# Mixture-of-experts stage: a new order of the expert units, gate-up weights stored in 4 KB runs, the next large unit's first two weight tiles split ahead of the down products, and the casts of y queued behind them

## The chip, the cores and the metric

The kernel runs on one core of a Trainium2 chip, in one launch. The metric is the device time of that launch in microseconds, the median over several runs. One further run was taken by the hardware profiler, and its trace is what all durations below come from. The engines are named as in the profile: PE is the matrix engine and PEld its weight load, DVE the vector engine, ACT the scalar engine, POOL and SP the other two; SPq is SP's queue of transfers.

## The reference

A block of transformer layers runs on 256 tokens of width 1024 in float32 (two feed-forward layers, a hybrid mixer, memory attention, convolution and differential attention). It ends with a mixture of experts, which the change is about:

```python
def moe_ffn(h, w_router, router_bias, w_gu, w_down, w_sh_gu, w_sh_down):
    ...
    _, eidx = lax.top_k(jnp.where(emask, choice, -jnp.inf), TOP_K)
    ...
    def chunk(args):
        tc, gc = args
        g, u = jnp.split(jnp.einsum('td,edf->tef', tc, w_gu), 2, axis=-1)
        return jnp.einsum('tef,efd->td', jax.nn.silu(g) * u * gc[..., None], w_down)
    ...
    sg, su = jnp.split(t @ w_sh_gu, 2, axis=-1)
    shared = (jax.nn.silu(sg) * su) @ w_sh_down
    return (routed + shared).reshape(B, S, D)
```

There are 64 experts of inner width 256, each token goes to 8 of them, and one shared expert takes all tokens. One expert has 2 MB of gate-up weights (1024 x 512) and 1 MB of down weights (256 x 1024).

## The kernel before, in words

The expert stage (`experts`) works through 27 units. A unit of kind L is one expert with up to 128 tokens; S is two experts with up to 64 tokens each; Q is four experts with up to 32 each (unit Q6 has two); the first, X, is three experts whose weights are known before the routing is done. Behind X come 14 L, 5 S and 7 Q units, 50 experts in all.

A unit multiplies its tokens `xe` by the gate-up weights into `eg` (eight slices of 128 rows, two to a tile), applies the gated activation (`glu`: `es` on ACT, then on DVE, and a transpose to `ehT` on PE), multiplies by the down weights into `y` (two halves `b` of 512 columns), and adds `y` to the four accumulators `acc`. That adding is a scatter by a 0/1 matrix `GT`: `y` is split into a high part `yh` (ACT) and a low part `yl` (DVE), and PE multiplies both, eight matmuls for a unit. They are kept in `self.left` and issued inside the next unit's `glu`, ahead of its transpose.

S and Q units use the float32 weights as they are. An L unit runs with split weights: ACT casts each tile of 1024 columns into `whi`, DVE subtracts it into `wlo` (`split`, by `wsplit`; four buffers of each), and PE does three matmuls for each slice (hi by hi, hi by lo, lo by hi: lines 2111 to 2113 for `eg`, 2124 to 2126 for `y`). For every second unit of a kind the tokens are gathered once for two units (`slots`, 32 matmuls `gx`, and `gg`, `GT`); the gather for unit q+1 is issued in unit q, between its transpose and its down products (`ahead`).

Weights arrive in tiles of 512 KB, six for an expert: four of gate-up and two of down (`expert_weights`, line 2054). A down tile is 128 rows of 4 KB; a gate-up tile has two runs of 2 KB for each partition, because its two slices lie 256 KB apart in memory. SP issues all of them in the order of the units, for the experts of a unit in turn, and waits where the buffer is not free. `raw` hands out the buffers in a fixed cycle of 20 (`RAW_N`), which is less than the 24 tiles of a Q unit. A tile of an S or Q unit is free when PE has read it, one of an L unit when both halves of its split are done.

The order of the units is computed from `SEQL`; it is X Q S Q L L S L Q L L Q L S L L Q L L S L Q L L L S Q. Behind the last unit the accumulators are scaled by `gB` and added to the residual, and the result is stored.

In program order a unit's weights are asked for and split at its own beginning, which is behind the casts of the unit before. The scheduler may move instructions of one engine against each other within the limits that `issue_after` sets.

Of the kernel before, what the change touches and what calls it, by code (L numbers as in the profile page):

```python
# [8 lines left out]
F32, F32R, I32 = dt.float32, dt.float32r, dt.int32  # L9
# [5 lines left out]
P = 128  # L15
# [6 lines left out]
NL, NS, NQ, NX = 14, 10, 26, 3  # L22
# [3 lines left out]
NRAW, WX, LB, LAST = 4, 6, 1, 4  # L26
CNORM = 1
ADA, ADA_BUFS, ADA_AHEAD = (10, 2), 3, 2
SEQL = (0.16, 0.7, 0.2, 0.0)

RAW_X = ["wx"] * WX + ["gB"] * 3 + ["xn"] * 3 + ["xel"] * 2 + ["xeh"] * 2 + ["xT"] * 2
RAW_1 = ["wraw"] * 2 + ["xT"] * 2 + ["wraw"] * 2
# [76 lines left out]
    return w.reshape(8, P, 1024)  # L109


def _freqs():
    import numpy as np

    return np.power(500000.0, -np.arange(0, 16, 2) / 16.0).astype(np.float32)[None]


class Net:
# [47 lines left out]
        return t  # L166

    def split(self, hi, lo, src, eng=None):
        self.nc.scalar.copy(hi, src)  # L169
        (eng or self.nc.vector).tensor_sub(lo, src, hi.bitcast(F32))  # L170

    def transpose_split(self, src, hi, lo, t, full=None):

# [134 lines left out]
    def wsplit(self, raw, eng=None, more=None):  # L308

        kc, n = raw.shape[1:]  # L310
        out = []
        st = min(kc, max(1, 1024 // n))
        for c in range(0, kc, st):
            if more is None:
                hi = self.whi.tile([P, st, n], F32R, name="whi", tag="whi")
                lo = self.wlo.tile([P, st, n], F32R, name="wlo", tag="wlo")
            else:
                hi, lo = [more[0].tile([P, st, n], F32R, name="wmore", tag=more[1], bufs=more[2]) for _ in range(2)]
            self.split(hi, lo, raw[:, c : c + st], eng)
            out += [(hi[:, i], lo[:, i]) for i in range(st)]  # L320
        return out

# [1722 lines left out]
    def expert_weights(self, es):  # L2045

        nc, A = self.nc, self.A
        out = [[] for _ in es]
        for i in range(6):
            for j, e in enumerate(es):  # L2050
                w = self.raw([P, 2, 512] if i < 4 else [P, 1, D])
                W, o = (A["w_exp_gu_2"], 2 * i) if i < 4 else (A["w_exp_down_2"], i - 4)
                src = W[0][bass.ds(e, 1)].rearrange("o (c p) n -> p (o c) n", p=P)
                dma = nc.sync.dma_start(w, src[:, o : o + w.shape[1]])
# [22 lines left out]
    def add_left(self):  # L2077
        left, self.left = self.left, []
        with self.tc.issue_after(self.last.ins):
            for f in left:  # L2080
                self.last = f()
# [7 lines left out]
    def scatter(self, y, b, GT, acc, last, r=P, first=False):  # L2089

        nc = self.nc
        yh, yl = self.ysplit(y, r)

        def add():
            for t in range(2):
                g = GT[:r, t * P : (t + 1) * P]
                nc.tensor.matmul(acc[t][b], g, yh, start=first, stop=False)  # L2097
                mm = nc.tensor.matmul(acc[t][b], g, yl, start=False, stop=last)  # L2098
            return mm

        self.left.append(add)

    def unit_L(self, w, xe, gate, put, ahead):
# [15 lines left out]
        with self.tc.issue_after(self.last.ins):  # L2119
            for b in range(2):  # L2120
                y = self.psum("y")
                o = slice(b * 512, b * 512 + 512)
                for c, (hi, lo) in enumerate(wd):
                    nc.tensor.matmul(y, hh[:, c], hi[:, o], start=c == 0, stop=False)
                    nc.tensor.matmul(y, hh[:, c], lo[:, o], start=False, stop=False)
                    nc.tensor.matmul(y, hl[:, c], hi[:, o], start=False, stop=c == 1)
                put(b, y)

    def unit_cols(self, pmT, gT, Sel, Off, tag):

# [16 lines left out]
        self.split(gU[:, :, :, 0], gU[:, :, :, 1], pv)  # L2147
        return Pu, gU

    def unit_multi(self, ws, n, xe, gate, put, ahead):  # L2150
# [11 lines left out]
        with self.tc.issue_after(self.last.ins):  # L2162
            for b in range(2):
                y = self.psum("y")
                for c in range(2):
                    for i, w in enumerate(ws):
                        o = slice(n * i, n * i + n)
                        nc.tensor.matmul(y[o], hT[:, c, o], w[4 + c][:, 0, b * 512 : b * 512 + 512],  # L2168
                                         start=c == 0, stop=c == 1)
                put(b, y)  # L2170

    def experts(self, h2t, U, fixed, shared):
        ids, Pu, gU = U["ids"], U["Pu"], U["gU"]
        nS, nQ = (NS + 1) // 2, (NQ + 3) // 4

        seq = [(SEQL[0] + (i + 0.5) / NL * SEQL[1], "L", i) for i in range(NL)]
        seq += [((i + SEQL[2]) / nS, "S", i) for i in range(nS)]

        seq += [((i + 1.0) / nQ if i < nQ - 1 else SEQL[3], "Q", i) for i in range(nQ)]
        seq = [("X", 0)] + [q[1:] for q in sorted(seq)]  # L2180
        first = dict(L=0, S=4 * NL, Q=Q0)
        cnt = dict(L=NL, S=nS, Q=nQ)
        ready = {("X", 0): U["X"]}

        def slots(q):

            if q == len(seq):
                return
            kind, i = seq[q]
            if i % 2 == 0:  # L2190
# [3 lines left out]
        self.left = []  # L2194

        def ahead(q):
            if q == 1:
                shared(acc)
            slots(q + 1)

        for q, (kind, i) in enumerate(seq):
            last = q == len(seq) - 1
            u0 = first.get(kind, 0) + 4 * i
# [3 lines left out]
            GTj, gate = GT[:, j], gs[:, j : j + 1]  # L2207
            if kind == "L":
                w = self.expert_weights(self.expert_ids(ids, [u0]))[0]
                self.unit_L(w, xj, gate, lambda b, y: self.scatter(y, b, GTj, acc, last), lambda: ahead(q))  # L2210
            else:
                n, k = dict(S=(64, min(NS - 2 * i, 2)), Q=(32, min(NQ - 4 * i, 4)), X=(32, NX))[kind]
                ws = fixed if kind == "X" else self.expert_weights(
                    self.expert_ids(ids, [u0 + n // 32 * v for v in range(k)]))
                self.unit_multi(ws, n, xj[0], gate,
                                lambda b, y: self.scatter(y, b, GTj, acc, last, n * k, q == 0), lambda: ahead(q))
        for f in self.left:
            f()
        self.left = []
# [2 lines left out]
    def overflow(self, h2t, U, gB):  # L2222
# [21 lines left out]
        with tc.For_i(0, total):  # L2244
# [33 lines left out]
            self.unit_L(w, [x[:, :, :P] for x in xe], gs[:, 0:1], put, lambda: None)  # L2278
            self.store()
            nc.vector.tensor_scalar(cnt, cnt, 1.0, None, ALU.add)  # L2280

# [43 lines left out]
norm2_g_2 w_router_2 router_bias_2 w_exp_gu_2 w_exp_down_2 w_sh_gu_2 w_sh_down_2""".split()  # L2325
_STAGES = ("ffn1", "mix", "mem", "ffn2", "blk", "moe")


# [21 lines left out]
```

## Time and profile before

| | |
|---|---|
| three runs | 1457.02, 1455.15, 1456.77 us; median 1456.77 us |
| the profiled execution | 1449.17 us |
| its span, first to last instruction | 1447.4 us |
| X unit's first matmul to the last scatter matmul's end | 1018.2 to about 1437.4 us |
| busy in the span: PE, DVE, ACT | 95%, 62%, 46% |
| SP queue's packets, as a share of 16 transfer engines' time | 70.8% |

The table is read from the profile's first page. Between the 1447.4 us of the span and the 1449.17 us of the execution lie 1.8 us outside the first and last instruction. The expert stage takes 419 us of the span, so its average is not that of the page: in that stretch the transfer engines are busy nearly all the time, and DVE less than half.

### The profile page before, as it was taken

How to read it: one execution, taken by the hardware profiler on the slowest of the kernel's cores; microseconds unless marked ns; L12 is line 12 of the kernel's file. 1: busy time of each engine (PE TensorE's matmuls, PEld its weight loads, DVE VectorE, ACT ScalarE, POOL GpSimd, SP SyncE). 2: the span in 40 equal slices, each digit the busy share in tenths (PEclk: the TensorE clock that was granted, in tenths of full speed). 3: DMA queues.
4: the chain of work that ended last, by engine and by line, in shares of the span. 5: the costliest groups of instructions: out<-in, count | busy, mean ns of one | idle time of the engine just before them, and what ended most of it. 6: DMA issues, size and time to landing. Idle time of an engine off the chain costs nothing.

```text
span 1447.4 us, 23621 instructions
## 1 busy us (share of the span) xinstructions
PE 1372.0 (95%) x8921; PEld 1078.0 (74%) x8921; DVE 899.2 (62%) x1420; ACT 666.2 (46%) x1051; POOL 128.1 (9%) x111
## 2 busy tenths in 40 slices
PE   6999999999999899999999989999999999989997
PEld 4999877898777679998798768776456575656572
DVE  4878465774457388664669987768226464645462
ACT  5445455545345354444453455843125353544351
POOL 1000012110101020000200314113000000000000
PEclk9999999999999999999999999999999999999999
DMA  7888566343245269875677543467989999999997
GB/s 263 293 301 288 191 205 206 98 138 103 74 161 185 78 229 309 271 245 184 201 238 219 153 130 89 159 211 270 372 299 395 394 390 396 391 392 385 340 383 266
DMA packets 175924, 358.00 MB, mean 247 GB/s; under 512 B 16099, under 2 KB 53931, under 8 KB 175807
## 3 DMA queue, kind: packets, MB, share of 16 engines
q1 hardware_dynamic: 175807, 356.46, 70.8%
q8 instruction: 71, 1.16, 0.3%
q14 instruction: 46, 0.38, 0.1%
HBM read 354.81 MB, written 1.60 MB: 246 GB/s over the span
## 4 chain that ended last, share of the span: by engine, by line
PE 55%; DVE 4%; ACT 3%; issue 1%; POOL 0%; DVEq 0%; POOLq 0%; ACTq 0%
PE eg L2158 6%; PE gx L2009 4%; PE y L2168 4%; PE lw L377 2%; PE eg L2112 2%; PE acc L2097 2%; PE lw L375 2%; PE lw L376 2%; PE eg L2113 2%; PE eg L2111 2%; PE acc L2098 2%; DVE wlo L170 2%; PE u L564 1%; PE g L565 1%; PE u L565 1%; PE g L564 1%
## 5 line engine op out<-in xcount | busy, mean ns | idle before, releaser
L170 DVE TENSOR_TENSOR wlo<-wraw,whi 128x1024 fp32r<-128x1024 f32 x262 | 323.3, 1244 | 120.7 <-ACT whi L169 119.5
L169 ACT CAST whi<-wraw 128x1024 fp32r<-128x1024 f32 x264 | 275.3, 1049 | 245.6 <-PE lw L377 54.8
L170 DVE TENSOR_TENSOR yl<-y,yh 128x512 fp32r<-128x512 f32 (+2 forms) x54 | 37.0, 689 | 74.9 <-ACT yh L169 74.9
L564 PE MATMUL u<-xTh,whi 128*128 128x256 f32 x288 | 82.1, 285 | 0.0
L2158 PE MATMUL eg<-wx,xe 128*32 128x512 f32 (+1 forms) x520 | 81.9, 594 | 0.0
L564 PE MATMUL g<-xTh,whi 128*128 128x256 f32 x288 | 81.6, 283 | 0.0
L565 PE MATMUL g<-xTl,whi 128*128 128x256 f32 x288 | 81.5, 283 | 0.0
L566 PE MATMUL g<-xTh,wlo 128*128 128x256 f32 x288 | 81.5, 283 | 0.0
L566 PE MATMUL u<-xTh,wlo 128*128 128x256 f32 x288 | 81.5, 283 | 0.0
L565 PE MATMUL u<-xTl,whi 128*128 128x256 f32 x288 | 81.5, 283 | 0.0
L170 DVE TENSOR_TENSOR wlo<-wx,whi 128x1024 fp32r<-128x1024 f32 x62 | 73.4, 1220 | 8.8 <-ACT whi L169 8.1
L1298 DVE SCALAR_TENSOR_TENSOR aacc<-wada,cc,aacc 128x1024 f32<-128x1024 f32 x48 | 61.5, 1281 | 18.2 <-DMA wada<-in_w_ada 17.5
L2066 DVE SCALAR_TENSOR_TENSOR es<-es,gsl,eg 128x256 f32<-128x256 f32 (+2 forms) x27 | 12.9, 479 | 85.5 <-ACT es L2065 85.5
L169 ACT CAST whi<-wx 128x1024 fp32r<-128x1024 f32 x62 | 63.1, 1051 | 5.2 <-PE eg L2113 3.2
L2158 PEld LDWEIGHTS eg<-wx,xe 128*32 128x32 f32 (+1 forms) x520 | 23.6, 117 | 50.7 <-issue 46.0
L169 ACT CAST yh<-y 128x512 fp32r<-128x512 f32 (+2 forms) x54 | 31.5, 586 | 62.6 <-PE y L2168 35.8
L2065 ACT ACTIVATE es<-eg 128x256 f32<-128x256 f32 (+2 forms) x27 | 10.4, 385 | 105.2 <-PE eg L2158 85.8
L2009 PE MATMUL gx<-G,h2h 128*128 128x256 f32 (+1 forms) x240 | 57.8, 284 | 0.0
L564 PEld LDWEIGHTS u<-xTh,whi 128*128 128x128 f32 x288 | 55.2, 192 | 3.4 <-ACT sf L537 1.7
L377 PE MATMUL lw<-whi,hl 128*128 128x512 f32 x144 | 56.7, 394 | 0.0
L2009 PE MATMUL gx<-G,h2l 128*128 128x256 f32 (+1 forms) x240 | 56.5, 278 | 0.0
L376 PE MATMUL lw<-wlo,hh 128*128 128x512 f32 x144 | 56.4, 392 | 0.0
(699 smaller groups left out, 3703.8 us busy)
## 6 DMA issues: line engine op xcount, KB each, us to landing
wx<-in_w_exp_gu SPq DMA_DIRECT2D x170, 512.0 KB
wx<-in_w_exp_down SPq DMA_DIRECT2D x86, 512.0 KB
wraw<-in_w_in SPq DMA_DIRECT2D x84, 512.0 KB
wada<-in_w_ada SPq DMA_DIRECT2D x48, 512.0 KB
wraw<-in_ffn_w_gate SPq DMA_DIRECT2D x44, 512.0 KB
wraw<-in_ffn_w_up SPq DMA_DIRECT2D x44, 512.0 KB
wraw<-in_ffn_w_down SPq DMA_DIRECT2D x44, 512.0 KB
wraw<-in_w_exp_gu SPq DMA_DIRECT2D x42, 512.0 KB
```

The costliest lines, as they stand in the source:

```text
L169: self.nc.scalar.copy(hi, src)
L170: (eng or self.nc.vector).tensor_sub(lo, src, hi.bitcast(F32))
L375: nc.tensor.matmul(o, x[0], w[0], start=start, stop=False)
L376: nc.tensor.matmul(o, x[0], w[1], start=False, stop=False)
L377: return nc.tensor.matmul(o, x[1], w[0], start=False, stop=stop)
L564: nc.tensor.matmul(p, hi, xh[:, k], start=k == 0, stop=False)
L565: nc.tensor.matmul(p, hi, xl[:, k], start=False, stop=False)
L566: mm = nc.tensor.matmul(p, lo, xh[:, k], start=False, stop=k == K - 1)
L1298: nc.vector.scalar_tensor_tensor(acc, w, self.cc[:, k : k + 1], acc, ALU.mult, ALU.add)
L2009: nc.tensor.matmul(ps[:, i * n : (i + 1) * n], h[:, t, f], G[:, t], start=j == 0, stop=j == 3)
L2158: mm = nc.tensor.matmul(ps[o], xe[:, k, o], w[k // 2][:, k % 2], start=k == 0, stop=k == 7)
L2168: nc.tensor.matmul(y[o], hT[:, c, o], w[4 + c][:, 0, b * 512 : b * 512 + 512], start=c == 0, stop=c == 1)
```

## The change

Four things change, all in the expert stage.

The **order** of the units is now written out as a string: X Q Q S L L Q L L S L L Q L S L Q L L L S L Q L S L Q. The numbers of units are the same.

**Gate-up weights** are passed to the kernel in another layout (`_pairs`): the two slices of a tile lie side by side, so that a tile is 128 rows of 4 KB, as a down tile is. The bytes are the same.

**A unit's weights are asked for in the unit before** (`then`, called ahead of the down products). If the next unit is an L, its first two gate-up tiles are split there as well, and the casts of this unit's `y` are issued behind those two splits (`split_first`).

**One of the four scatter pieces** (two matmuls) is held back until the transpose has been issued, in units behind which no gather follows (`behind`).

```diff
+SEQ = "QQSLLQLLSLLQLSLQLLLSLQLSLQ"
...
+def _pairs(w):
+    e, k, n = w.shape
+    return np.ascontiguousarray(w.reshape(e, k // 256, 2, P, n).transpose(0, 1, 3, 2, 4).reshape(e, k // 256, P, 2 * n))
...
     def expert_weights(self, es):
...
+                if i < 4:
+                    src = A["exp_gu"][bass.ds(e, 1), i].rearrange("o p (c n) -> p (o c) n", c=2)
...
     def glu(self, ps, mm, gate, r, ahead):
...
-        self.add_left()
+        self.add_left(len(self.left) - self.behind)
         pt = self.psum("ehT")
         with self.tc.issue_after(self.last.ins):
             for c in range(2):
                 self.last = nc.tensor.transpose(...)
+        self.add_left(len(self.left))
...
     def scatter(self, y, b, GT, acc, last, r=P, first=False):
-        yh, yl = self.ysplit(y, r)
+        with ExitStack() as es:
+            for i in self.split_first:
+                es.enter_context(self.tc.issue_after(i.ins))
+            yh, yl = self.ysplit(y, r)
...
+        self.left += [lambda t=t: add(t) for t in range(2)]
...
     def unit_L(self, w, ws, xe, gate, put, ahead, then):
         for k in range(0, 8, 2):
-            for i, (hi, lo) in enumerate(self.wsplit(w[k // 2])):
+            for i, (hi, lo) in enumerate(ws[k // 2] if k // 2 < len(ws) else self.wsplit(w[k // 2])):
...
         wd = self.wsplit(w[4]) + self.wsplit(w[5])
+        then()
+        for b in range(2):
+            with self.tc.issue_after(self.last.ins):
...
+            self.last = mm
+            put(b, y)
...
     def experts(self, h2t, U, fixed, shared):
...
+        def then(q):
+            self.split_first = ()
+            if q < len(seq):
+                kind, i = seq[q]
+                n, k = size(kind, i)
+                ws = self.expert_weights(self.expert_ids(ids, [...]))
+                weights[q] = ws, [self.wsplit(ws[0][v]) for v in range(2)] if kind == "L" else []
+                self.split_first = self.halved if kind == "L" else ()
         for q, (kind, i) in enumerate(seq):
+            self.behind = 0 if q < 2 or gathers(q + 1) else 1
+            ws, split = weights.pop(q)
...
```

How the change moves instructions is shown at three places. The first is ACT at the fourth full Q unit and the L unit behind it (Q3 and L8 in both orders). Before, from the Q unit's gather on:

```order
L2161 COPY ehT<-ehT 128x256
L169 CAST xeh<-gx 128x512 x4
L2035 CAST GT<-GT 128x512
L169 CAST yh<-y 128x512 x2
L169 CAST whi<-wx 128x1024 x6
L2065 ACTIVATE es<-eg 128x256
```

and now:

```order
L2177 COPY ehT<-ehT 128x256
L178 CAST xeh<-gx 128x512 x4
L2043 CAST GT<-GT 128x512
L178 CAST whi<-wx 128x1024 x2
L178 CAST yh<-y 128x512 x2
L178 CAST whi<-wx 128x1024 x4
L2075 ACTIVATE es<-eg 128x256
```

Two of the L unit's six casts stand ahead of the two casts of the Q unit's `y`, which PE has to finish first; DVE's subtractions stand in the same order.

The second is PE at the same L8 and the L9 behind it, where no gather stands between. Before, from the last scatter pieces to the first gate-up matmuls of L9:

```order
L2097 MATMUL acc<-yh,GT 128x512
L2098 MATMUL acc<-yl,GT 128x512
L2072 MATMUL ehT<-ident,es 128x128 x2
L2124 MATMUL y<-whi,ehh 128x512
L2125 MATMUL y<-wlo,ehh 128x512
L2124 MATMUL y<-whi,ehh 128x512
L2125 MATMUL y<-wlo,ehh 128x512
L2111 MATMUL eg<-whi,xeh 128x512
L2112 MATMUL eg<-wlo,xeh 128x512
L2126 MATMUL y<-whi,ehl 128x512
```

and now:

```order
L2082 MATMUL ehT<-ident,es 128x128 x2
L2111 MATMUL acc<-yh,GT 128x512
L2112 MATMUL acc<-yl,GT 128x512
L2139 MATMUL y<-whi,ehh 128x512
L2140 MATMUL y<-wlo,ehh 128x512
L2141 MATMUL y<-whi,ehl 128x512
L2139 MATMUL y<-whi,ehh 128x512
L2140 MATMUL y<-wlo,ehh 128x512
```

Two scatter matmuls stand between the transpose and the first product now, and the third product, which needs the low part `ehl`, stands third instead of fifth; L9's `eg` no longer stands among them.

The third is SP, at the weights of the X unit, up to the first load of an expert's number behind them. Before and now:

```order
L2054 DMA wx<-in_w_exp_gu 128x2x512 x2
L2054 DMA wx<-in_w_exp_down 128x1024 x2
L2054 DMA wx<-in_w_exp_gu 128x2x512 x6
L2054 DMA wx<-in_w_exp_down 128x1024 x4
L442 DMA wraw<-in_w_sh_down 128x1024 x2
L2039 TENSOR_LOAD ids
```

```order
L2064 DMA wx<-in_exp_gu 128x1024 x2
L2064 DMA wx<-in_w_exp_down 128x1024 x2
L2064 DMA wx<-in_exp_gu 128x1024 x6
L2064 DMA wx<-in_w_exp_down 128x1024 x4
L450 DMA wraw<-in_w_sh_down 128x1024 x2
L2047 TENSOR_LOAD ids
```

A gate-up tile is read as rows of 1024 words where it was two rows of 512; the order of the transfers changes only with that of the units.

## Rows read from the trace of the kernel before

**Rows 1.** Expert stage by --windows: length, busy of PE, PEld, DVE, ACT, POOL, PEclk, DMA, GB/s

```profile
1018.20:1437.40 419.20, 399.53 (x2285) 251.31 (x2285) 191.10 (x265) 164.39 (x249) 0.00 (x0) 0.99 1.00 375
```

**Rows 2.** PE's waits in the expert stage: us in total, times, longest

```profile
PE eg L2111 <- ACT whi L169: 7.6, 4, 2.2
PE eg L2112 <- DVE wlo L170: 3.8, 5, 0.8
PE y L2124 <- ACT ehh L169: 3.7, 8, 0.5
PE y L2168 <- ACT ehT L2161: 2.3, 5, 0.5
```

**Rows 3.** The longest wait for an arriving weight tile in the same stretch

```profile
ACT whi L169 <- DMA wx<-in_w_exp_down: 1.5, 3, 1.0
```

**Rows 4.** Chain of waits, Q3 and the start of L8: start, us, what

```profile
1271.30 7.00 PE eg L2158 x64
...
1280.58 3.77 PE gx L2009 x32
...
1285.20 3.75 PE y L2168 x32
...
1289.42 0.59 ACT yh L169
1290.01 0.95 ACT whi L169
...
1290.98 1.24 DVE wlo L170
...
1293.01 0.43 PE eg L2113
...
1296.41 0.23 PE eg L2113
```

**Rows 5.** By --windows, the start of L8

```profile
1292.00:1296.00 4.00, 3.74 (x9) 2.96 (x10) 3.78 (x5) 2.84 (x3) 0.00 (x0) 0.57 1.05 402
```

**Rows 6.** Chain pieces: the down products of Q1, Q2 and Q5

```profile
1156.06 7.23 PE y L2168 x31
...
1207.71 4.74 PE y L2168 x32
...
1429.97 5.76 PE y L2168 x31
```

**Rows 7.** Timeline at L0 to L1: DVE, then PE: start, us, instruction

```profile
1101.08 0.48 DVE L2066 SCALAR_TENSOR_TENSOR es<-es,gsl,eg 128x256 f32<-128x256 f32 x1 [0.20 <-ACT es L2065]
1102.01 1.22 DVE L170 TENSOR_TENSOR wlo<-wx,whi 128x1024 fp32r<-128x1024 f32 x1 [0.45 <-ACT whi L169]
1103.15 0.42 DVE L170 TENSOR_TENSOR ehl<-ehT,ehh 128x256 fp32r<-128x256 f32 x1
...
1103.17 0.50 PE L2124 MATMUL y<-whi,ehh 128*128 128x512 f32 x1 [0.46 <-ACT ehh L169]
```

**Rows 8.** By --windows: gate-up tiles arrive in the first, down tiles in the others

```profile
1132.00:1148.00 16.00, 15.54 (x79) 9.62 (x79) 10.88 (x13) 8.74 (x12) 0.00 (x0) 1.00 1.05 387
1151.00:1159.00 8.00, 7.54 (x54) 3.66 (x48) 0.48 (x1) 0.76 (x2) 0.00 (x0) 1.00 1.03 410
...
1201.00:1209.00 8.00, 7.54 (x62) 3.16 (x58) 0.48 (x1) 0.76 (x2) 0.00 (x0) 1.00 1.03 405
```

**Rows 9.** By --windows: stretches in which the transfers ran slow, and a full one

```profile
1052.00:1060.00 8.00, 8.00 (x51) 3.98 (x51) 3.60 (x7) 2.33 (x4) 0.00 (x0) 1.00 0.23 73
1060.00:1082.00 22.00, 22.00 (x152) 10.80 (x152) 4.09 (x8) 3.69 (x7) 0.00 (x0) 1.00 1.00 351
1330.00:1361.00 31.00, 30.54 (x201) 18.49 (x202) 14.15 (x21) 11.90 (x18) 0.00 (x0) 1.00 0.88 319
1400.00:1421.00 21.00, 20.54 (x115) 11.20 (x117) 4.15 (x10) 4.60 (x10) 0.00 (x0) 1.00 1.00 358
...
1082.00:1330.00 248.00, 234.63 (x1310) 155.63 (x1299) 127.54 (x170) 109.69 (x161) 0.00 (x0) 0.99 1.04 393
```

More of the change, by code (lines that the diff above doesn't have):

```diff
@@ L28 @@
 ADA, ADA_BUFS, ADA_AHEAD = (10, 2), 3, 2
-SEQL = (0.16, 0.7, 0.2, 0.0)
+SEQ = "QQSLLQLLSLLQLSLQLLLSLQLSLQ"
 RAW_X = ["wx"] * WX + ["gB"] * 3 + ["xn"] * 3 + ["xel"] * 2 + ["xeh"] * 2 + ["xT"] * 2
@@ L2075, in glu, with add_left @@
         return pt[:, : 2 * r].rearrange("p (c s) -> p c s", c=2)
-    def add_left(self):
-        left, self.left = self.left, []
+    def add_left(self, n):
+        left, self.left = self.left[:n], self.left[n:]
         with self.tc.issue_after(self.last.ins):
@@ L2091, in scatter, with add, unit_L @@
         nc = self.nc
-        yh, yl = self.ysplit(y, r)
[L2094 to L2103, printed above, removed]
+        with ExitStack() as es:
+            for i in self.split_first:
+                es.enter_context(self.tc.issue_after(i.ins))
+            yh, yl = self.ysplit(y, r)
+        def add(t):
+            g = GT[:r, t * P : (t + 1) * P]
+            nc.tensor.matmul(acc[t][b], g, yh, start=first, stop=False)
+            return nc.tensor.matmul(acc[t][b], g, yl, start=False, stop=last)
+        self.left += [lambda t=t: add(t) for t in range(2)]
+    def unit_L(self, w, ws, xe, gate, put, ahead, then):
         nc, mp = self.nc, self.mp
@@ L2118, in unit_L @@
         wd = self.wsplit(w[4]) + self.wsplit(w[5])
[L2119 to L2122, printed above, removed]
+        then()
+        for b in range(2):
+            y = self.psum("y")
+            o = slice(b * 512, b * 512 + 512)
+            with self.tc.issue_after(self.last.ins):
                 for c, (hi, lo) in enumerate(wd):
@@ L2125, in unit_L @@
                     nc.tensor.matmul(y, hh[:, c], lo[:, o], start=False, stop=False)
-                    nc.tensor.matmul(y, hl[:, c], hi[:, o], start=False, stop=c == 1)
-                put(b, y)
+                    mm = nc.tensor.matmul(y, hl[:, c], hi[:, o], start=False, stop=c == 1)
+            self.last = mm
+            put(b, y)
     def unit_cols(self, pmT, gT, Sel, Off, tag):
@@ L2148, in unit_cols, with unit_multi @@
         return Pu, gU
-    def unit_multi(self, ws, n, xe, gate, put, ahead):
+    def unit_multi(self, ws, n, xe, gate, put, ahead, then):
         nc, mp = self.nc, self.mp
@@ L2161, in unit_multi @@
         nc.scalar.copy(hT[:, :, :r], pt)
-        with self.tc.issue_after(self.last.ins):
-            for b in range(2):
-                y = self.psum("y")
+        then()
+        for b in range(2):
+            y = self.psum("y")
+            with self.tc.issue_after(self.last.ins):
                 for c in range(2):
@@ L2167, in unit_multi @@
                         o = slice(n * i, n * i + n)
-                        nc.tensor.matmul(y[o], hT[:, c, o], w[4 + c][:, 0, b * 512 : b * 512 + 512],
-                                         start=c == 0, stop=c == 1)
-                put(b, y)
+                        mm = nc.tensor.matmul(y[o], hT[:, c, o], w[4 + c][:, 0, b * 512 : b * 512 + 512],
+                                              start=c == 0, stop=c == 1)
+            self.last = mm
+            put(b, y)
     def experts(self, h2t, U, fixed, shared):
@@ L2174, in experts @@
         nS, nQ = (NS + 1) // 2, (NQ + 3) // 4
[L2176 to L2180, printed above, removed]
+        num = dict(L=iter(range(NL)), S=iter(range(nS)), Q=iter([nQ - 1, *range(nQ - 1)]))
+        seq = [("X", 0)] + [(k, next(num[k])) for k in SEQ]
         first = dict(L=0, S=4 * NL, Q=Q0)
@@ L2185, in slots @@
         def slots(q):
[L2187 to L2190, printed above, removed]
+            if gathers(q):
+                kind, i = seq[q]
                 ready[kind, i // 2] = self.slots(h2t, Pu, gU, first[kind] + 4 * i, min(2, cnt[kind] - i), kind)
@@ L2194, in experts @@
         self.left = []
+        gathers = lambda q: q < len(seq) and seq[q][1] % 2 == 0
         def ahead(q):
@@ L2199, in ahead @@
             slots(q + 1)
+        size = lambda kind, i: dict(L=(P, 1), S=(64, min(NS - 2 * i, 2)), Q=(32, min(NQ - 4 * i, 4)), X=(32, NX))[kind]
+        weights, self.split_first = {0: (fixed, [])}, ()
+        def then(q):
+            self.split_first = ()
+            if q < len(seq):
+                kind, i = seq[q]
+                n, k = size(kind, i)
+                ws = self.expert_weights(self.expert_ids(ids, [first[kind] + 4 * i + n // 32 * v for v in range(k)]))
+                weights[q] = ws, [self.wsplit(ws[0][v]) for v in range(2)] if kind == "L" else []
+                self.split_first = self.halved if kind == "L" else ()
         for q, (kind, i) in enumerate(seq):
             last = q == len(seq) - 1
-            u0 = first.get(kind, 0) + 4 * i
+            self.behind = 0 if q < 2 or gathers(q + 1) else 1
             xe, GT, gs = ready[kind, i // 2]
@@ L2207, in experts @@
             GTj, gate = GT[:, j], gs[:, j : j + 1]
+            n, k = size(kind, i)
+            ws, split = weights.pop(q)
+            put = lambda b, y: self.scatter(y, b, GTj, acc, last, n * k, q == 0)
+            more = lambda: ahead(q), lambda: then(q + 1)
             if kind == "L":
-                w = self.expert_weights(self.expert_ids(ids, [u0]))[0]
-                self.unit_L(w, xj, gate, lambda b, y: self.scatter(y, b, GTj, acc, last), lambda: ahead(q))
-            else:
[L2212 to L2216, printed above, removed]
+                self.unit_L(ws[0], split, xj, gate, put, *more)
+            else:
+                self.unit_multi(ws, n, xj[0], gate, put, *more)
         for f in self.left:
@@ L2276, in put @@
                     nc.vector.tensor_add(self.h[:, t, s], self.h[:, t, s], v)
-            self.unit_L(w, [x[:, :, :P] for x in xe], gs[:, 0:1], put, lambda: None)
+            self.behind = 0
+            self.unit_L(w, [], [x[:, :, :P] for x in xe], gs[:, 0:1], put, lambda: None, lambda: None)
             self.store()
```

17 lines of the change are left out of this document (9 added, 8 removed).

## Prediction

> **What bounds the kernel now.** I read the page first: PE is busy 95% of the span and the transfers are not, so PE looks like the only bound. By stages it is otherwise. In the expert stage, which alone the change touches, PE is busy 399.53 of 419.20 us and the transfer engines 1.00 of the time at 375 GB/s [rows 1]. Both are nearly full, and the price of an edit has to be worked out on each side.
>
> PE's side is read from its waits. Four times the first gate-up matmul of an L unit waits for its cast (7.6 us), five times the second for its subtraction (3.8 us), and 13 times the first down product waits for the transposed activation, 0.46 us each (3.7 and 2.3 us) [rows 2]. The chain shows the first kind at Q3 to L8: the down products end, ACT casts `yh`, and only then `whi`, and DVE subtracts, while PE stands still [rows 4]. The tiles were there: ACT's casts waited for arriving tiles for 1.5 us in all, and no wait for a tile is longer [rows 3].
>
> The busy time hides more. The 32 down products of Q3 take 3.75 us [rows 4], those of Q1 7.23, of Q2 4.74 and of Q5 5.76 [rows 6]: PE there works through tiles as they arrive, and the page calls it busy. And behind the standstill at L8 the granted clock is 0.57 over 4 us [rows 5], at the 1.2 GHz level for most of it: matmuls are 0.43 us apart and then 0.23 [rows 4], which is the 2.4 GHz level. L3 shows the same.
>
> The transfers' side is read in windows. While gate-up tiles arrive the rate is 387 GB/s, while down tiles arrive 410 or 405 [rows 8]. Both are 512 KB tiles of 128 rows; they differ in 2 KB against 4 KB runs. And in four stretches the rate falls below the 393 of a full one: to 73, 351, 319 and 358 [rows 9], since all buffers are full and SP waits for PE.
>
> **The change part by part, PE's side.**
>
> Splits ahead. Two of six casts of an L unit move ahead of the casts of `y`, and their subtractions likewise. What stood on PE's path there, 7.6 + 3.8 = 11.4 us [rows 2], goes where the tiles are in. A Q unit with a gather gives ACT and DVE the gather and 3.75 us of products to do two splits, 0.95 and 1.24 us for the first [rows 4]. The moved casts of `y` cost PE nothing by themselves: the scatter that reads them comes behind 24 `eg` matmuls of 0.23 us, 5.6 us later. Behind the standstills the clock doesn't fall: at L8 and L3 some 8 matmuls at 0.43 instead of 0.23, 1.6 us each, 3.2 together.
>
> The held-back scatter piece. Two matmuls of 0.23 us fill the 0.46 us behind the transpose. The new order, too, has 13 units without a gather behind them. In nine of them this removes 9 x 0.46 = 4.1 us. In the other four an L follows an L, and there DVE does the next unit's subtraction before `ehl`: `ehl` ends 2.5 us after the start of `es` [rows 7], while PE, now without its gap, wants it for the third product. In the row the first product starts at 1103.17; without the gap it starts 0.46 earlier, and the third 2 x 0.23 later, so at 1103.17 against `ehl`'s end at 1103.57. I take 0.4 us lost in each of the four against the 0.46 gained: nothing. Bounds: 1.8 us better, 1.8 worse.
>
> Weights asked for one unit earlier in program order: SP's queue issues the tiles in the order of the units as before, and its waits are for buffers, so I cost this at nothing; the cover is the transfers already queued ahead.
>
> PE without waiting for tiles gains 11.4 + 3.2 + 4.1 = 18.7 us. Over Q3's 3.75 us the products of Q1, Q2 and Q5 lost 3.5 + 1.0 + 2.0 = 6.5 us to arriving tiles [rows 4, 6]. If these went as well, PE would end 25.2 us sooner.
>
> **The transfers' side.** The 50 experts behind X have 200 gate-up tiles of 524,288 bytes. At 387 GB/s one takes 1.355 us, at the 407.5 of a down tile 1.287 [rows 8]: 0.068 x 200 = 13.6 us. The slow stretches lost 8 x (1 - 73/393) = 6.5 us, and then 2.4, 5.8 and 1.9 us [rows 9]. The first stays: it lies at the shared expert's products, which only PE's pace ends. The other 10.1 us can shrink. So the last tile can land 13.6 to 23.7 us sooner.
>
> The Trainium skill has a rule that speaks for less here: "DMA: Bandwidth & Descriptors", Why small descriptors are slow, gives a fixed overhead of about 3 cycles per packet, at 32 bytes a cycle otherwise: 64 cycles for 2 KB and 128 for 4 KB. By it, as an estimate, the longer run would be worth 2.2% of the rate, some 6 us; the trace shows 5% between the two kinds of tile, and the measurement decides.
>
> The order. Counted from Q to Q, the old one has 54, 36, 54, 54 and 54 tiles to bring behind Q0, the new one 48, 60, 48, 60 and 48. At 1.287 us that is 62 or 77 us. PE needs, without waits, 10.7 us for an L (24 + 12 + 8 matmuls of 0.23, and 0.5 for the transpose), 13 for an S or Q (7.0 and 3.75 [rows 4], the scatter and the transpose), 4.6 for a gather (from 1280.58 to 1285.20 [rows 4]): 56 us for the first piece, 82 for the second, 56, 82, and 52 for the last. So the transfers fall behind by 6 us and regain 5, in turn, and twenty buffers hold 26 us of them. Only in the last piece do they lose 10. I therefore take two thirds of the 6.5 us of late tiles, 4.3, as gone, and the rest as staying at the end.
>
> **Sum.** 18.7 + 4.3 = 23.0 us; I take 1.4 off for standstills that the tighter stage shows anew (half of the 0.59 + 0.95 + 1.24 us that one Q-to-L change costs in [rows 4]). That leaves 21.6 us, which is inside what the transfers allow. The profiled execution of 1449.2 us would become 1427.6 us. The median of the runs shown, 1456.8 us, lies 7.6 us above that execution, and I carry the gain over unchanged: **1435.2 us**.
>
> **Rivals.**
>
> *The run length is not what separates 387 from 405 and 410.* Then the transfers gain only the 10.1 us of idle stretches, and lose some back in the tighter pieces: the end moves 7 to 12 us, 1447 us. For it: no run here shows a gate-up tile in 4 KB runs. Against: the down tiles have the same size and queue, and only the runs and their distance differ. By the Trainium skill's overhead per packet (above) it would come out in between, some 6 us better than this.
>
> *It fits better than I take it.* All late tiles and all idle stretches go: 25.2 us from PE's side and 23.7 from the transfers', 1432 us, and down to 1428 with the upper bound at `ehl` and 410 GB/s throughout.
>
> *The change gives back what it gains, through the order.* Three L units in a row with an S and an L behind them (L8 to L11) fill the buffers, the transfers idle as at 1330 [rows 9], and the Q units pay. If each of the five Q units behind Q0 lost Q1's 3.5 us [rows 6], 17.5 us would be owed, against 6.5 now: of the 18.7 us 7.7 are left, and if the transfers' rate stays as well, nothing: 1457 us.
>
> *Slower: casts pinned behind a tile that is late.* If the first two tiles of an L come after the Q unit's products have ended, ACT and DVE stand at those splits with the casts of `y` queued behind them. PE then waits for the tile, 0.95 us of cast and 1.24 of subtraction [rows 4], and the scatter follows later: 2.2 us plus the lateness for one such place. The 18.7 us are lost if each of the 14 L units pays 1.5 us more than now; at 2 us it would be 1463 us. For it: with tiles arriving just in time at Q1 and Q5 [rows 6] the next unit's are later still. Against: late tiles were waited for only 1.5 us at the casts [rows 3], and the transfers get faster.
>
> That the scheduler doesn't do as told is excluded by the order shown.
>
> **How the numbers follow.** My forecast, a gain of 17 to 24 us, has 0.59; the better fit 0.14; the unchanged rate 0.17; the order giving it back 0.05; the pinned casts 0.05. About 0.2%, 2.9 us, is what a measurement of this kernel can tell from no change. The forecast, the better fit and the unchanged rate are faster, 0.90; the order's case splits between faster and same; so 0.91 faster, 0.04 same, 0.05 slower. The range 1428 to 1448 takes in the first three cases with their bounds, 0.90 less their tails.
>
> **What would show it.** The profile after should have: gate-up windows at 400 GB/s or more; no wait of `eg` on `whi` above 1 us at the Q-to-L changes, and PEclk 1.00 there; `yh` casts behind two `whi` on ACT; waits of `y` on `ehT` gone; a wait of `y` on `ehl` of about 0.4 us at L-to-L; down products of 3.8 us in all Q units but the last. The prediction is wrong if gate-up tiles still come at 387, or if new waits of PE on tiles exceed 6 us.

## The result, and the profile after

| | before | after |
|---|---|---|
| median, first set of runs | 1455.96 us (4 runs) | 1437.24 us (4 runs) |
| ratio, 95% interval | | 0.989 (0.986 to 0.9919) |
| ratio in a second set, 5 rounds | | 0.9899 (0.9862 to 0.9936) |
| profiled execution | 1449.17 us, span 1447.4 us | 1434.7 us, span 1432.9 us |
| first product of X to first `xn` of the end | 419.20 us | 404.95 us |

The change is faster by 1.0 to 1.1%: 18.7 us between the medians of the first set, 14.8 in the second (1451.86 to 1437.09). The profiled pair differs by 14.5 us, of which 14.25 lie in the expert stage. Executions of one kernel spread by more than 10 us, and the longer ones have the lower mean granted clock: the 18 of the kernel before in the second set go from 1448.1 us (0.989) to 1464.4 us (0.979). Line numbers are some 8 to 17 higher in the changed kernel: `split` is L178, the `eg` products of an L unit L2125 to L2127, its `y` L2139 to L2141, `eg` and `y` of S and Q units L2174 and L2185.

Windows of the changed kernel, with the columns of [rows 1]: the whole expert stage, two stretches at and behind the shared expert's products, then two stretches with the order's long pieces and a full one between.

```profile
1018.59:1423.54 404.95, 399.22 (x2287) 246.53 (x2286) 191.39 (x265) 164.35 (x249) 0.00 (x0) 1.00 0.98 387
...
1050.00:1060.00 10.00, 10.00 (x79) 6.32 (x79) 3.57 (x7) 2.92 (x5) 0.00 (x0) 1.00 0.35 123
...
1060.00:1070.00 10.00, 10.00 (x77) 5.35 (x72) 0.63 (x3) 1.34 (x3) 0.00 (x0) 1.00 1.00 381
...
1190.00:1220.00 30.00, 30.00 (x216) 20.92 (x218) 13.64 (x23) 11.57 (x19) 0.00 (x0) 1.00 0.91 359
1220.00:1330.00 110.00, 108.67 (x586) 70.46 (x580) 61.84 (x80) 53.09 (x78) 0.00 (x0) 1.00 1.03 409
1330.00:1365.00 35.00, 35.00 (x242) 23.47 (x239) 17.29 (x27) 15.37 (x24) 0.00 (x0) 1.00 0.94 371
```

Against [rows 1], PE's busy time is the same (399.53 and 399.22 us), so by these rows the gain is standstill: 19.7 us before, 5.7 after. The rate of a full stretch is 409 GB/s, where it was 393 [rows 9]. The granted clock is 1.00 throughout.

PE's waits in that stage, to be held against [rows 2]: us in total, times, longest.

```profile
PE eg L2126 <- DVE wlo L178: 2.1, 4, 0.6
PE ehT L2082 <- DVE es L2076: 1.1, 1, 1.1
PE y L2141 <- DVE ehl L178: 0.8, 4, 0.2
PE y L2185 <- DMA wx<-in_w_exp_down: 0.5, 2, 0.2
```

The waits of `eg` on `whi` (7.6 us) and of `y` on `ehh` and `ehT` (3.7 and 2.3 us) are gone, and the four short waits on `ehl` have come. But there is another kind of wait, which PE's own rows hide, because a matmul whose weights are late counts as busy. It shows at the weight loads (PEld) and at the casts. First the kernel before, the waits for arriving tiles in the expert stage, beside which stands [rows 3]:

```profile
PEld eg L2158 <- DMA wx<-in_w_exp_down: 1.5, 5, 0.3
PEld y L2168 <- DMA wraw<-in_w_exp_down: 1.1, 4, 0.3
PEld eg L2158 <- DMA wx<-in_w_exp_gu: 0.6, 2, 0.3
```

The changed kernel, the same view, ACT's largest row and four of the weight loads:

```profile
ACT whi L178 <- DMA wx<-in_exp_gu: 4.8, 4, 2.1
...
PEld eg L2174 <- DMA wx<-in_exp_gu: 4.6, 10, 1.1
PEld y L2185 <- DMA wx<-in_w_exp_down: 4.1, 5, 1.2
...
PEld y L2185 <- DMA wraw<-in_w_exp_down: 2.2, 2, 1.1
...
PEld y L2185 <- DMA wx<-in_exp_gu: 0.6, 2, 0.3
```

Late tiles cost the weight loads 3.2 us before and, with two smaller rows, 12.4 after. The chain says the same. In the kernel before it ran over PE to the end of Q5's products [rows 6]; in the changed kernel it runs through transfers at Q1 to L2, at Q3 to L8 and over the whole end. Chain of waits of the changed kernel, Q1 to L2 and the end:

```profile
1125.93 10.22 DMA wx<-in_exp_gu
...
1136.23 1.05 ACT whi L178
...
1137.31 1.01 DVE wlo L178
...
1408.45 10.04 DMA wraw<-in_w_exp_down
...
1418.54 1.10 PE y L2185 x6
...
1419.66 3.76 DMA gB<-modr
...
1423.54 1.89 DVE xn L1787 x3
```

The last down products wait for the last tiles, and nothing of PE's is in the way. (`gB`, by which the accumulators are scaled, stands behind them on the chain because its transfer waits for a buffer that they free; it lands at 1423.42 us, and the last scatter matmul ends at 1423.43.)

### The profile page after: what moved, and what is told of

Its sections match the earlier page's. It is cut to its first block, busy times and chain, and to the rows that moved or that the text cites. A ratio compares the mean times of both kernels' runs of the same rounds, so it can differ in the third digit from the quotient of the medians.

```text
span 1432.9 us, 23632 instructions
## 1 busy us (share of the span) xinstructions
PE 1369.5 (96%) x8921; PEld 1072.5 (75%) x8921; DVE 899.8 (63%) x1420; ACT 665.8 (46%) x1051; POOL 127.9 (9%) x111
## 4 chain that ended last, share of the span: by engine, by line
PE 39%; DVE 10%; DMA 9%; ACT 2%; issue 2%; POOL 1%; SPq 0%; DVEq 0%; POOLq 0%; ACTq 0%
PE eg L2174 4%; DMA wx<-in_exp_gu 4%; DVE cy L1467 3%; PE gx L2017 3%; DMA wx<-in_w_exp_down 3%; DVE wlo L178 3%; PE lw L385 2%; PE y L2185 2%; PE lw L383 2%; PE lw L384 2%; DMA wraw<-in_exp_gu 1%; PE u L572 1%; PE g L573 1%; PE g L572 1%; PE g L574 1%
## 5 line engine op out<-in xcount | busy, mean ns | idle before, releaser
L178 DVE TENSOR_TENSOR wlo<-wraw,whi 128x1024 fp32r<-128x1024 f32 x248 | 306.9, 1246 | 118.9 <-ACT whi L178 116.7
L178 ACT CAST whi<-wraw 128x1024 fp32r<-128x1024 f32 x250 | 261.2, 1049 | 245.1 <-PE lw L385 55.4
L178 DVE TENSOR_TENSOR wlo<-wx,whi 128x1024 fp32r<-128x1024 f32 x76 | 89.8, 1220 | 18.7 <-ACT whi L178 17.9
L2174 PE MATMUL eg<-wx,xe 128*32 128x512 f32 (+1 forms) x480 | 82.9, 595 | 0.3 <-DMA wx<-in_exp_gu 0.2
L178 ACT CAST whi<-wx 128x1024 fp32r<-128x1024 f32 x76 | 76.9, 1049 | 8.0 <-DMA wx<-in_exp_gu 4.8
L178 DVE TENSOR_TENSOR yl<-y,yh 128x512 fp32r<-128x512 f32 (+2 forms) x54 | 36.6, 687 | 43.7 <-ACT yh L178 43.7
L2174 PEld LDWEIGHTS eg<-wx,xe 128*32 128x32 f32 (+1 forms) x480 | 22.9, 116 | 46.4 <-issue 40.7
L383 PE MATMUL lw<-whi,hh 128*128 128x512 f32 x144 | 56.2, 390 | 0.0
```

The lines of the kernel that those rows point to most:

```text
L178: return self.nc.scalar.copy(hi, src), (eng or self.nc.vector).tensor_sub(lo, src, hi.bitcast(F32))
L383: nc.tensor.matmul(o, x[0], w[0], start=start, stop=False)
L2174: mm = nc.tensor.matmul(ps[o], xe[:, k, o], w[k // 2][:, k % 2], start=k == 0, stop=k == 7)
```

## Experiments

Theory A, from these rows: the changed kernel has two bounds that lie within a few us of each other. PE has little standstill left, and the transfers, whose queue stands idle now and then because all buffers are full, set the end. Then each part of the change is worth something only as long as the other bound allows it. The rivals: one side alone made the gain.

Every run below computes everything. Two numbers are given for each: the ratio to the kernel before from the timed rounds, and the length of the expert stage in the one profiled execution, from the start of the last `sh` product ahead of X to the first `xn` at the end. The second leaves out what lies ahead of that stage, which moved by up to 10 us between executions (that `sh` product began at 1013.3 us in one and at 1023.7 in another). It is one execution for each kernel, and the two of the change differ by 1.6 us. Before it is 421.8 us (1015.6 to 1437.40), after 407.5 (1016.0 to 1423.54).

| kernel | ratio, 95% interval | stage, us |
|---|---|---|
| before | 1 | 421.8 |
| 4 KB runs alone | 0.9998 (0.997 to 1.0027) | 419.7 |
| change, no pin | 0.9944 (0.9914 to 0.9973) | 418.8 |
| change, 2 KB runs | 0.9946 (0.9926 to 0.9967) | 416.6 |
| change, no split ahead | 0.9956 (0.9931 to 0.9981) | 414.2 |
| change, old order | 0.9914 (0.9891 to 0.9937) | 409.9 |
| change, none held back | 0.9889 (0.9848 to 0.9929) | 409.0 |
| change | 0.989 (0.986 to 0.9919) | 407.5 |
| change, once more | 0.9899 (0.9862 to 0.9936) | 409.1 |
| shared products in Q0 | 0.9846 (0.9803 to 0.9889) | 404.9 |
| the same, once more | 0.9851 (0.9821 to 0.9882) | 406.5 |
| even order | 0.9893 (0.986 to 0.9926) | 406.6 |
| even order, shared products in Q0 | 0.9856 (0.9825 to 0.9888) | 401.9 |

### The run length, taken back

```diff
-                if i < 4:
-                    src = A["exp_gu"][bass.ds(e, 1), i].rearrange("o p (c n) -> p (o c) n", c=2)
...
+                W, o = (A["w_exp_gu_2"], 2 * i) if i < 4 else (A["w_exp_down_2"], i - 4)
+                src = W[0][bass.ds(e, 1)].rearrange("o (c p) n -> p (o c) n", p=P)
```

> The change with its gate-up tiles read in 2 KB runs again (order, splits ahead and pin stay). Theory A, two bounds: the changed kernel ends with its transfers, so 200 gate-up tiles at 1.355 instead of about 1.282 us cost 14.6 us of transfer time, of which 8 to 14 show: 1445 to 1451 us. Rival B, TensorE's order made the gain and the run length is not the cause: 1435 to 1439 us, with the chain at the end still on TensorE.

Measured: 1444.03 us, 0.9946; the stage is 9.1 us longer than the change's. Windows of this kernel, the second to be held against the 409 of the change:

```profile
1070.00:1190.00 120.00, 117.41 (x621) 72.94 (x621) 66.18 (x87) 55.95 (x82) 0.00 (x0) 1.00 1.04 393
1220.00:1330.00 110.00, 107.98 (x579) 68.60 (x579) 61.20 (x80) 51.67 (x75) 0.00 (x0) 1.00 1.04 394
```

The rate is back at 393 to 394 with nothing altered but the layout, and the late gate-up tiles at PE's loads grow from 4.6 us to this:

```profile
PEld eg L2172 <- DMA wx<-in_w_exp_gu: 12.3, 16, 1.2
```

So the layout does set the rate, and in the changed kernel it is worth 7.5 to 9 us of stage and 0.5 to 0.6% of the time, 7 to 8 us. The length of the runs and the distance between the two runs of a tile changed together, and no run tells them apart. The time is at the low end of what theory A gave or just below it, and too much for rival B, which falls: the other parts of the change alone make about half of the gain.

### The run length alone

The kernel before with the new layout of the gate-up weights, that is the other direction of the diff above.

> The kernel before with 4 KB gate-up runs alone. Theory A: TensorE still stands still at every way into a large unit (about 13 us of its 19.7 us), only the waits for late tiles go: 3 to 7 us faster than before, 1449 to 1453 us. Rival C, the run length is the whole gain: 14 to 19 us faster, 1437 to 1442 us. Rival B, it is nothing: 1455 to 1457 us.

Measured: 1450.88 us against 1450.95, no difference to 0.3%. By the times rival B (nothing) came true, and theory A's 3 to 7 us were missed; the interval leaves only 3 to 4 of them possible. Its pieces show why. Chain pieces of this kernel, the down products of Q1, Q2 and Q5, beside [rows 6]:

```profile
1154.64 4.62 PE y L2178 x32
...
1202.20 3.80 PE y L2178 x30
...
1426.82 5.17 PE y L2178 x32
```

They sum to 13.6 us where they were 17.7: the late tiles did shrink, by 4.1 us. But PE's waits on its own casts are as before (7.7 us for `whi`), its standstill is 19.7 us still, and behind the gap at Q2 to L5 the clock now falls where it had been full:

```profile
1016.60:1433.68 417.08, 397.38 (x2285) 251.53 (x2285) 190.99 (x266) 163.96 (x249) 0.00 (x0) 0.99 0.96 376
1210.00:1215.00 5.00, 5.00 (x13) 3.94 (x12) 3.92 (x4) 2.47 (x3) 0.00 (x0) 0.50 1.02 407
```

The stage is 2.1 us shorter. The rest of the faster transfers was spent standing idle: the share falls from 1.00 [rows 1] to 0.96 at nearly the same rate, 376 GB/s against 375.

### The old order

```diff
-SEQ = "QQSLLQLLSLLQLSLQLLLSLQLSLQ"
+SEQ = "QSQLLSLQLLQLSLLQLLSLQLLLSQ"
```

> The change with the order of units of the kernel before (X Q6 S0 Q0 L0 L1 S1 L2 Q1 ...); 4 KB runs, splits ahead and pin stay. Theory A as the prediction has it: the late tiles at Q1, Q2 and Q5, 4.3 us of 6.5, come back, partly smaller for the faster tiles: 1 to 5 us slower than the change, 1438 to 1442 us. Rival D, the order is most of the gain: over 8 us slower, above 1445 us. Rival E, the order is worth nothing once tiles come faster: within 1 us.

Measured: 1438.08 us, 0.9914, stage 409.9 us. By the trace the order is worth 1 to 2.5 us, as expected, and by the ratios 2 to 3.5; the intervals overlap, so the runs speak against rival D (most of the gain) and leave E (nothing) possible. With the old one the casts of two L units wait long for tiles:

```profile
ACT whi L178 <- DMA wx<-in_exp_gu: 10.2, 4, 7.0
ACT whi L178 <- DMA wraw<-in_exp_gu: 4.6, 2, 4.3
```

Most of these 14.8 us are not PE's: ACT stands at tiles that PE doesn't need yet, and no wait of `eg` on `whi` is left in PE's rows.

### No split ahead

```diff
-                weights[q] = ws, [self.wsplit(ws[0][v]) for v in range(2)] if kind == "L" else []
-                self.split_first = self.halved if kind == "L" else ()
+                weights[q] = ws, []
```

> The change with the next large unit's tiles split only at its own start again, so nothing is pinned either; order and 4 KB runs stay. Theory A: the 11.4 us of waits on the splits and the clock drops (3.2 us) return on TensorE, which has 5.7 us of standstill left in the changed kernel: 8 to 14 us slower, 1445 to 1451 us. Rival F, the transfers alone set the end now and hide the splits: 0 to 3 us slower, 1437 to 1440 us.

Measured: 1445.21 us, 0.9956, 0.6 to 0.7% above the change, 8 to 10 us; the stage is 5 to 7 us longer. The waits are nearly those of [rows 2] again:

```profile
PE eg L2125 <- ACT whi L178: 6.8, 4, 1.7
PE eg L2126 <- DVE wlo L178: 3.8, 5, 0.8
```

Rival F falls: the transfers don't hide the splits. They hide a part, since late tiles at PE's loads fall from 12.4 to 8.0 us when PE is slower.

### No pin

```diff
-                self.split_first = self.halved if kind == "L" else ()
```

> The change without the pin: the tiles are still split ahead, but the casts of y need not stay behind them on ScalarE (at Q to L they then stand between the two casts of the tile, at Q3 to L8 ahead of both). Theory A: the first split of a few large units is late by a cast of y, 0.6 to 1.2 us at three to seven places: 1 to 5 us slower than the change. The prediction's slow rival (pinned casts wait behind a late tile and cost): up to 3 us faster than the change. Rival F (transfers set the end): within 1 us of it.

Measured: 1446.4 us, 0.9944, 0.45 to 0.54% above the change, 6.5 to 8 us, and more than I had expected. The waits are to the digit those of the kernel without any split ahead: `whi` 6.8 us in four, `wlo` 3.8 in five. The timeline of ACT at Q3 to L8 in this kernel shows it:

```profile
1293.35 0.58 ACT L178 CAST yh<-y 128x512 fp32r<-128x512 f32 x1 [1.37 <-PE y L2185]
1295.07 0.58 ACT L178 CAST yh<-y 128x512 fp32r<-128x512 f32 x1 [1.13 <-PE y L2185]
1295.55 3.89 ACT L178 CAST whi<-wx 128x1024 fp32r<-128x1024 f32 x4
```

Here ACT stood still for 1.37 and 1.13 us in front of casts of `y`, with the tile's cast behind them. In the changed kernel, at S0 to L0, the order is the other one:

```profile
1091.51 2.00 ACT L178 CAST whi<-wx 128x1024 fp32r<-128x1024 f32 x2
1093.40 0.59 ACT L178 CAST yh<-y 128x512 fp32r<-128x512 f32 x1
```

At Q to L the split ahead in program order alone gives nothing; the pin carries it.

That the stage is 4.6 us longer here than without any split ahead is mostly the clock. In this trace it falls at three places of the stage, near 1148, 1237 and 1299 us, in the other at one, near 1138, each time behind a wait of `eg` on `whi` and `wlo`. A window of 4 us shows about 0.6 there, mostly the 1.2 GHz level, which costs some 1.6 us. One window of this kernel, and the one of the kernel without the split ahead:

```profile
1236.00:1240.00 4.00, 4.00 (x13) 3.09 (x12) 4.00 (x4) 2.34 (x4) 0.00 (x0) 0.57 1.03 410
...
1137.00:1141.00 4.00, 3.97 (x10) 3.12 (x11) 4.00 (x4) 2.61 (x3) 0.00 (x0) 0.57 1.03 410
```

The timed ratios, 0.9944 and 0.9956, don't tell the two kernels apart.

### No piece of the scatter held back

```diff
-            self.behind = 0 if q < 2 or gathers(q + 1) else 1
+            self.behind = 0
```

> The change with no piece of the scatter held back until the transpose (behind = 0 everywhere). The prediction's term was 9 places of 0.46 us, 4.1 us: with theory A the transfers take up a part of it, so 1 to 4 us slower than the change, with the waits of y on ehT and ehh back in the trace. Rival F (transfers set the end): within 1 us of the change.

Measured: 1437.21 us against 1437.09 for the change in the same set; stage 409.0 us against 409.1 and 407.5. The waits are back, and cost nothing:

```profile
PE y L2139 <- ACT ehh L178: 4.2, 9, 0.5
PE y L2185 <- ACT ehT L2177: 1.8, 4, 0.5
```

Their 6 us are taken from time that PE would otherwise spend at tiles (10.5 us at its loads against 12.4) and at `ehl`. For this term rival F holds, and theory A's 1 to 4 us did not come.

### The idle stretch of the queue, removed

In the changed kernel the queue stands idle from 1051 to 1058 us. By its own waits, SP stands there for the `y` products of Q6:

```profile
SPq L2064 <- PE y L2185: 12.3, 2, 11.9
```

Those come late because the shared expert's products and a gather lie ahead of them. The edit moves the products one unit on:

```diff
         def ahead(q):
-            if q == 1:
+            if q == 2:
                 shared(acc)
```

> The change with the shared expert's down products (24 products, about 6 us of TensorE, in which no weight buffer comes free) put into the unit Q0 instead of Q6; all else stays. In the changed kernel the queue stands idle for 6.5 us at 1051 to 1058 us with every buffer full, and starts again when the y of Q6 frees four. Theory A, transfers set the end: that idle stretch goes, the last tile lands up to 6.5 us sooner, and TensorE's own work (400.9 us of 406.6) bounds the gain: 2 to 5 us faster than the change. Theory G, TensorE's work sets the end and the transfers only keep up with it: within 1 us of the change.

Measured: 1431.13 us against 1437.09 for the change in the same set, 0.9846 against 0.9899; in another set 0.9851. The stage is 404.9 and 406.5 us in the two executions of this kernel, against 407.5 and 409.1 in those of the change, 2.6 us shorter in the mean. Windows, the first two to be held against 123 and 359 in the change:

```profile
1050.00:1060.00 10.00, 10.00 (x80) 3.16 (x76) 0.69 (x2) 0.96 (x2) 0.00 (x0) 1.00 0.82 281
1190.00:1220.00 30.00, 30.00 (x222) 20.00 (x221) 13.54 (x23) 12.36 (x21) 0.00 (x0) 1.00 0.86 337
```

Of the idle 7.0 us in the first (10 x (1 - 123/409)) 3.9 go, and 1.6 come back in the second: the buffers fill up later instead. The chain at Q1 to L2 is PE's now, and the last tiles still set the end:

```profile
1405.12 10.06 DMA wraw<-in_w_exp_down
...
1415.22 1.10 PE y L2185 x6
```

Nothing that PE computes was made shorter, only a queue started earlier. Theory G (PE sets the end) would have it within 1 us, and both sets speak against that. This kernel has the lowest medians measured here: it is faster than before in both sets, and 0.4 to 0.5% below the change by both, though the intervals still overlap.

> The change with the shared expert's down products in Q0, once more, as the reference for the next two on the same chip. Theory A: a ratio of 0.981 to 0.987 to the kernel before.

Measured: 1432.11 us, 0.9851, as expected.

### An even order

Both edits, the second without the move of the shared products:

```diff
-SEQ = "QQSLLQLLSLLQLSLQLLLSLQLSLQ"
+SEQ = "QQSLLQLLSLQLSLLQLSLLQLSLLQ"
```

> The shared products in Q0 and the units in an even order, 54 tiles from each Q to the next (Q Q S L L Q L L S L Q L S L L Q L S L L Q L S L L Q) instead of 48, 60, 48, 60, 48. The queue still stands idle with every buffer full for some 7 us in 1190 to 1220 and 1330 to 1365 us, after the long stretches. Theory A: these shrink by half, the last tiles land about 3 us sooner, and the 3 to 5 us of late tiles that TensorE still has go: 0 to 4 us faster than the change with the shared products in Q0. Theory G (TensorE's own work is all that is left there): within 1 us of it.

> The change with the even order (54 tiles from Q to Q) and the shared products where the change has them, in Q6. Theory A: the idle 6.5 us at 1051 to 1058 us stay, so it keeps most of the distance to the kernel with the shared products in Q0; the later idle stretches shrink: 1 to 4 us faster than the change, a ratio of 0.986 to 0.989 to the kernel before. Theory G: as the change, 0.9895.

Measured: 1435.11 us (0.9856) and 1439.36 us (0.9893). In the trace of the first the mechanism is there. Windows:

```profile
1190.00:1220.00 30.00, 28.96 (x191) 17.50 (x191) 12.83 (x19) 11.51 (x17) 0.00 (x0) 1.00 0.96 374
1330.00:1365.00 35.00, 33.98 (x233) 22.30 (x232) 14.64 (x23) 12.93 (x21) 0.00 (x0) 1.00 0.97 381
```

The slow stretches are at 374 and 381 GB/s, where the change has 359 and 371 and the first was at 337 with the shared products moved alone; the late tiles at PE's loads are 4.6 us instead of the change's 12.4, and the stage of 401.9 us is the shortest of all. But the timed ratios are those of the kernels with the uneven order, 0.9851 and 0.9890 to 0.9899, to their 0.3%: by the times both runs came out as theory G said. Whether the even order is worth its 3 us or more outside the one profiled execution stays open.

## Why the prediction was right in the total, and where it was not

The median after, 1437.2 us, lies 2.0 above the predicted 1435.2, and faster was the likeliest case. The gain itself was too large: 21.6 us predicted, 14.5 in the profiled pair, 14.8 and 18.7 in the medians.

That the total came so close is partly luck. The profiled execution after took 1434.7 us, 7.1 above the predicted 1427.6. But the median of the changed kernel lies only 2.5 us above its profiled execution, where the prediction carried over the 7.6 us of the kernel before, and this gives 5.1 us back. No step of the prediction worked that out, and such offsets need not come from the expert stage: the two profiled executions of the kernel with the shared products in Q0 took 1431.3 and 1441.1 us, and 8.4 of the 9.8 us between them lie ahead of X's first product (1018.0 and 1026.3 us). By the predicted steps:

**The splits ahead** (11.4 us): right. 11.4 us of waits became 2.1, all on `wlo`, and taking the splits or the pin away brings back 6.8 + 3.8 us of the waits and 5 to 10 us of time. The pinned-casts rival appeared in two places only, at Q1 to L2 and Q3 to L8, where `whi` stood at its tile; it was too small to turn the sign.

**The clock** (3.2 us): right; the drops are gone. In the thirteen traces the clock falls within the expert stage only where no splits are pinned ahead: at two places before, two with 4 KB runs alone, one without the split ahead and three without the pin, and at none in the nine others. The window at L8, where [rows 5] has 0.57:

```profile
1283.00:1287.00 4.00, 3.42 (x15) 2.79 (x16) 4.00 (x5) 2.35 (x4) 0.00 (x0) 1.00 1.03 410
```

**The held-back piece** (4.1 us): its waits went (6.0 us, against 0.8 new at `ehl`), but the run without it has the same time. The term was worth nothing, because late tiles took its place.

Up to here PE's standstill was to shrink by 11.4 + 4.1 - 1.4 = 14.1 us; it shrank by 19.67 - 5.73 = 13.9.

**The late tiles** are the step that failed: "I therefore take two thirds of the 6.5 us of late tiles, 4.3, as gone". PE's busy time, in which clock and late tiles lie, was to fall by 3.2 + 4.3 = 7.5 us and fell by 0.3. With the clock's 3.2 us gained, late tiles must have grown by some 2.9 us instead of shrinking by 4.3. These 7.2 us are nearly all that lies between 21.6 and the 14.25 of the stage.

The timelines agree. For the `eg` and for the `y` of every S and Q unit I take the time from the first start to the last end, and what it exceeds the shortest of its kind by (7.07 and 3.65 us). This sum is 6.8 us before and 10.1 in the changed kernel (0.9 at S0, 2.2 at Q1, 0.7 at Q3, 6.2 at Q5), 11.8 in its second execution. The order, on which the step relied, did not take late tiles away: the change with the old order has 10.1 us as well, at Q1, Q2, Q4 and Q5. Among the kernels with the longer runs the sum is 3.0 with these alone, 5.9 without the split ahead and 10.1 in the change: the less PE stands still between the units, the more it waits for tiles. The waits at the weight loads, 3.2 and 12.4 us, exaggerate the growth; at Q1 before, PE lost 3.5 us and the loads waited for tiles 0.9.

**The transfers' side** was worked out as a range, 13.6 to 23.7 us, and then not used as a bound. The rate came a little better than forecast: full stretches run at 409 GB/s, 1.282 us for a tile, so 200 tiles gain 14.6 us instead of 13.6. The idle stretches behind the first, 10.1 us, were said to be able to shrink, and I let them. They did so by a quarter: the windows above leave 10 x (1 - 381/409) + 30 x (1 - 359/409) + 35 x (1 - 371/409) = 7.6 us, and the first stayed as forecast (7.0 us, 6.5 before). By these sums the transfers gained 14.6 + 2.5 = 17.1 us. The timelines show less: the last tile came 15.3 us sooner (its weights are first loaded at 1433.82 before, and first multiplied at 1418.54 now), and Q5's products ended 14.4 us sooner (at 1435.72 and 1421.30). PEld and PE before, then PE now:

```profile
1433.82 0.14 PEld L2168 LDWEIGHTS y<-wraw,ehT 128*32 128x32 f32 x2 [0.24 <-DMA wraw<-in_w_exp_down]
...
1433.03 2.69 PE L2168 MATMUL y<-wraw,ehT 128*32 128x512 f32 x7
...
1412.56 1.99 PE L2185 MATMUL y<-wx,ehT 128*32 128x512 f32 x8
...
1418.54 0.62 PE L2185 MATMUL y<-wraw,ehT 128*32 128x512 f32 x1 [0.20 <-DMA wraw<-in_w_exp_down]
...
1419.87 1.43 PE L2185 MATMUL y<-wraw,ehT 128*32 128x512 f32 x3
```

"Inside what the transfers allow" meant inside the best case of a range, and the sum of PE's side should have been cut to near its lower end. Asking for the weights one unit earlier, which the prediction put at nothing, was not tried by itself.

The Trainium skill's rule on small descriptors ("DMA: Bandwidth & Descriptors", Why small descriptors are slow), some 3 cycles for each packet, would have given, as an estimate, 2.2% for the longer runs, and 1.5% in a stretch of which a third, the down tiles, was not changed. The runs decide against that figure: with 2 KB runs a full stretch has 393 GB/s and with 4 KB 409, which is 4%.

Of the signs named: gate-up stretches above 400 GB/s, no wait on `whi`, clock 1.00, the casts of `y` behind two `whi`, waits on `ehT` gone, all as said. The wait on `ehl` is 0.2 us each, half of the 0.4. "Down products of 3.8 us in all Q units but the last" holds for Q0, Q2 and Q4; Q1 and Q3 took 4.3 and 4.2 us by the timeline, and Q5 8.7. Of the signs of being wrong, new waits on tiles above 6 us, one reading came true: the waits at the weight loads grew by 9.2 us, though PE's own time at tiles grew by 3.3 to 5.0. One sum is off without bearing on the total: in the slow rival, 14 units at 1.5 us would take back 21 us, the whole forecast gain, and not the 18.7 of PE's side.

## What to carry to other kernels

Where PE and the transfers are both nearly full, work out the gain on each side and take the smaller, and of a range its low end; parts of a change then don't add up, and one that does nothing alone (the longer runs here) can be worth 7 to 8 us once the other side is out of the way. Look for late weights at the weight loads and in the length of the products as well, since a matmul that waits for its weights counted as busy here (399 us before and after). When the transfers have become the bound, look where their queue stands idle with full buffers: moving 6 us of PE work that frees no buffer into a unit that has just freed sixteen made 2.6 us of the stage here.

## What the hardware showed that I had not expected

The same 512 KB tiles, issued by the same queue into the same buffers, came at 393 to 394 GB/s in the full stretches with 2 KB runs among them, and at 404 to 409 with 4 KB runs, whichever other part of the change was in. Whether the length of the runs or their distance does it was not tried.

The clock is less regular than the prediction took it. With 4 KB runs alone it falls at two places, but not at L3 and L8 as before: it was 0.50 at 1210 to 1215 us, behind the gap at Q2 to L5, and 0.57 at 1362 to 1366. The kernel before has a gap of like length at the same place, 2.8 us of 15, and the clock stays full there:

```profile
1207.00:1222.00 15.00, 12.16 (x65) 7.03 (x64) 8.77 (x9) 7.93 (x10) 0.00 (x0) 1.00 1.04 391
```

The products ahead of that gap differ, 4.74 us of them at arriving tiles before [rows 6] and 3.80 with the faster ones; whether that is the cause was not tried.
